# Moving adaLN slabs into the projections, splitting the output projection, and dummy products at the start

## The chip, the cores and the metric

One core of a Trainium2 chip runs the whole kernel. The time is the device time of one execution in microseconds; the median of several runs counts. TensorE is PE, VectorE is DVE, ScalarE is ACT, GpSimd is POOL; SP is the engine whose queue issues most DMAs.

## The reference, cut to what matters

Two layers of a hybrid decoder, for one prompt of 512 tokens and eight samples of 4 tokens (544 columns in all), model width 1024:

```python
mod = silu(c) @ w_ada + b_ada                    # 1024 -> 6*1024, per sequence
sh1, sc1, g1, sh2, sc2, g2 = split(mod, 6)
h = rms_norm(x, norm1) * (1 + sc1) + sh1
proj = h @ w_in                                  # q 512 | k 128 | v 128 | u 256 | xr 256 | yg 256
o_attn = window_attention(q, k, v, sinks)        # 8 heads, window 128
o_ssm = s5(u);  o_lru = rglru(xr, yg)            # two recurrent branches, 256 wide each
o = concat(rms_norm(o_attn), rms_norm(o_ssm), rms_norm(o_lru))
x = x + g1 * (o @ w_o)
h2 = rms_norm(x, norm2) * (1 + sc2) + sh2
x = x + g2 * ffn(h2)                             # up 1024 -> 2*2816, causal conv, gelu * value, down
```

New caches and states are returned as well.

## The kernel before, in words

**Layout.** Features lie on partitions (8 tiles of 128), tokens on columns, in two halves: `HALF` 0 has 256 columns, half 1 has 288 (256 of the prompt and the 32 of the samples). A float32 product is made of three products of a split in two parts (`mm3`, L427): `whi*hh`, `whi*hl`, `wlo*hh`. Weights come in tiles of 128x8x128 (512 KB) by a DMA on SP into one of `NRAW` = 3 buffers `raw`; ACT casts them to `whi`, DVE subtracts to get `wlo`, into one of `NW` = 6 slots (`Weights.ahead`, L407). `weights_order` (L1601) sets the order in which tiles are fetched; a new tile is fetched when a slot is given back (`done`).

**adaLN.** `ada_slabs` (L491) makes `mod`. A slab is 128 rows of `w_ada` by 1024 columns (512 KB): four matmuls of 32 columns of the silu against 256 columns each, into four row groups of one bank. 8 slabs make a sum; then ACT copies it, two transposes turn it, DVE adds the bias. There are 6 such sums, 48 slabs, in a layer. A slab's load takes a `raw` buffer of the weights' three, but for four slabs at the start that go to spare tiles in pieces of 512 bytes. At the start of layer 0 the slabs of `sh1` and `sc1` (16) run ahead of everything, fetched up to 7 ahead. The other 32 of layer 0 and the first 16 of layer 1 run as a background generator (list `bg`) between the products of the mixers of layer 0, the last 32 of layer 1 between those of layer 1, fetched one ahead. `background()` advances it, once or more per `tick`.

**A layer.** `mixers` (L1442): the 12 column tiles of `w_in`, each 8 k by 2 halves by 3 = 48 products; the first three run as a group over k as their normalised inputs appear (`group`, L877). Each tile's result starts a chain (`Chains`): k and q (norm, rotary), v, the S5 branch `ssm_chain`, the RG-LRU branch `lru_chain`. Attention is made of 16 units per layer, one step of a unit per tick: `att_S` (scores, exp), `att_T` (transposes), `att_V` (times v). `proj` (L1535): o @ w_o for 8 column tiles i and two halves; k tiles 6, 7 are the RG-LRU branch, 4, 5 the S5 branch, 0 to 3 attention. Its first three tiles run as a group over k in the order `KO`, and `need(k, hf)` ticks until an input is there:

```python
o = [one(256, True) for i in range(GRP)]
for k in ko:
    need(k, 0)
    for i in range(GRP):
        mm3(o[i], W_[wn(i)], k, hs[k], HALF[0], k == ko[0], k == ko[-1])
```

After it the tiles go through all k at once, in an order that runs half 0 four tiles ahead of half 1 (`skewed`). `residual` evicts a sum into x on DVE. `ffn` (L1614): 44 tiles of the up-projection (48 products each, then `conv`, and per pair gelu and split), and the down-projection in three parts (`PARTS`). `finish` (L1653) and `down` call `background()` once a tile; there only `tables` of the next layer is in the list. `norm_half` (L850) normalises, scales, shifts and splits one half of x for all k.

PSUM has 8 banks: `wide` (two pairs) always, four singles `mb` in the mixers, one pair and two singles `fb` in the projections.

Of the kernel before, what the change touches and what calls it, by code (L numbers as in the profile page):

```python
# [19 lines left out]
L = 2  # L20
# [29 lines left out]
S3 = 1  # L50
# [13 lines left out]

PRM = {}
_n = 0
for _name, _w in (
# [10 lines left out]
    "wada": (L, 3, 8, 2, 128, 4, 256), "win": (L, 12, 128, 8, 128), "wo": (L, 8, 128, 8, 128),  # L78
# [56 lines left out]
def layout(I):  # L135
# [43 lines left out]
    A["wada"] = I["w_ada"].reshape(L, 8, 128, 3, 4, 2, 256).transpose(0, 3, 1, 5, 2, 4, 6)  # L179
# [137 lines left out]
def trunk(ctx: ExitStack, tc: tile.TileContext, A, O):  # L317
# [173 lines left out]
    def ada_slabs(l, banks, ahead, spare=()):  # L491
        d = LY[l]
        todo = [(bank, k, hf) for bank in banks for hf in range(2) for k in range(8)]
        have = {}

        def fetch(n):
            if n < len(todo) and n not in have:
                bank, k, hf = todo[n]
                if n in spare:
                    have[n] = [T(512) for _ in range(2)]  # L500
                    for a, t in enumerate(have[n]):
                        nc.sync.dma_start(t.rearrange("p (g c) -> p g c", g=4),
                                          A["wada"][l, bank, k, hf, :, :, 128 * a:128 * a + 128])
                    return
                raw = wp.tile([128, 8, 128], F32, tag="raw", name="raw", bufs=NRAW)
                have[n] = raw.rearrange("p (g a) c -> p g (a c)", g=4)
                nc.sync.dma_start(have[n], A["wada"][l, bank, k, hf])

        for n, (bank, k, hf) in enumerate(todo):
            for m in range(n, n + ahead + 1):  # L510
                fetch(m)
            if k == 0:
                if bank == 0 and hf == 0:
                    d["mod"] = lp.tile([128, 48, 9], F32, name="mod")
                ps = one(256)
            if n in spare:
                for a, t in enumerate(have[n]):
                    for g in range(4):
                        T_.matmul(ps[32 * g:32 * g + 32, 128 * a:128 * a + 128], silu[:, k, :],
                                  t[:, 128 * g:128 * g + 128], start=False, stop=k == 7, skip_group_check=True)  # L520
                free(*have[n])
            else:
                for g in range(4):
                    T_.matmul(ps[32 * g:32 * g + 32], silu[:, k, :], have[n][:, g],  # L524
                              start=k == 0, stop=k == 7, skip_group_check=True)
            del have[n]
            yield 1
            if k < 7:
                continue
            row = W(256)  # L530
            S.copy(row, ps)
            PS.put(ps)
            yield 1
            pt = one(256)
            for c in range(2):
                T_.transpose(pt[:, c * 128:c * 128 + 128], row[:, c * 128:c * 128 + 128], eye)

            def part(t):
                return t[:, bank * 16:bank * 16 + 16].rearrange("p (g h c) r -> p g h c r", g=4, h=2)[:, :, hf]

            src = pt.rearrange("p (c g r) -> p g c r", c=2, g=4)[:, :, :, 0:9]
            b = d["prm"]("bada")[:, :, None].to_broadcast([128, 48, 9])
            V.tensor_tensor(part(d["mod"]), src, part(b), op=OP.add)
            PS.put(pt)
            d["ada"] = (bank, hf)
            for al, at, bk in (("al1", 8, 0), ("al2", 32, 2)):
# [319 lines left out]
    def norm_all(hf, al, sh):  # L866
        yield from norm_stats(hf)
        for _ in norm_half(hf, al, sh):
            pass
# [942 lines left out]
```

## Time and profile before

| | |
|---|---|
| median of 3 runs (lowest, highest) | 1330.35 us (1328.3, 1334.8) |
| the profiled execution, and its span | 1335.0 us, 1333.2 us |
| PE busy, weight loads (PEld) busy | 1270.1 us (95%), 1164.8 us (87%) |
| DVE, ACT, POOL busy | 881.8 (66%), 576.5 (43%), 48.8 us (4%) |
| mean granted TensorE clock | 0.992 of full speed |
| DMA | 178.24 MB, mean 134 GB/s |

Stages by the span's time: start to 62 us, mixers of layer 0 to 245, its output projection to 305, its up- and down-projection to 690, mixers of layer 1 to 893, its output projection to 945, its up- and down-projection to the end. A matmul's duration holds the time to its end, some 0.28 us; in a run of products one starts every 0.12 to 0.13 us, so busy time can look full where products start rarely. Weight loads overlap matmuls and show that better. A float32 matmul that isn't split appears as two instructions.

### The profile page before, as it was taken

Reading aid. Unit: us, or ns where it says so; the run is one execution under the profiler, and the core shown is the slowest. Engines: PE = TensorE matmul, PEld = TensorE weight load, DVE = VectorE, ACT = ScalarE, POOL = GpSimd, SP = SyncE. Lnnn points to the kernel's source line nnn. Section 1 sums busy time; section 2 is a strip of 40 time slices with the busy share of each in tenths; the row PEclk is TensorE's granted clock in tenths of the full one; section 3 lists DMA queues with packets and bytes.
Section 4 is the critical chain, followed back from the end, with each engine's and each line's share of the span. In section 5 each row is a group of like instructions: output and inputs, shape, how many; then the busy total and the mean of one; then the engine's idle time right before and its main releaser. Section 6 shows DMA issues by size and latency. Waiting matters only on the chain.

```text
span 1333.2 us, 26368 instructions
## 1 busy us (share of the span) xinstructions
PE 1270.1 (95%) x10438; PEld 1164.8 (87%) x10438; DVE 881.8 (66%) x2583; ACT 576.5 (43%) x1112; POOL 48.8 (4%) x82
## 2 busy tenths in 40 slices
PE   4899988999999999999999999899999999999998
PEld 2666765799999999999998776679999999999998
DVE  8787885988774556456576877668865456545651
ACT  4557544356542343234354466545643234313430
POOL 0021010000020000000000001000000000000000
PEclk9899999999999999999999999999999999999999
DMA  8876677533343223334235846602322332233221
GB/s 294 279 265 215 191 252 229 178 111 118 93 135 125 85 86 87 97 93 115 76 108 180 268 142 203 191 14 90 110 81 86 96 95 74 86 97 94 85 72 51
DMA packets 72460, 178.24 MB, mean 134 GB/s; under 512 B 15584, under 2 KB 26752, under 8 KB 72336
## 3 DMA queue, kind: packets, MB, share of 16 engines
q1 hardware_dynamic: 65456, 162.08, 39.1%
q0 software_dynamic: 4960, 11.68, 2.5%
q10 hardware_dynamic: 1920, 2.79, 0.7%
q8 instruction: 82, 1.34, 0.4%
q14 instruction: 42, 0.34, 0.1%
HBM read 159.37 MB, written 14.34 MB: 130 GB/s over the span
## 4 chain that ended last, share of the span: by engine, by line
PE 83%; DMA 9%; DVE 5%; ACT 2%; issue 1%; POOL 0%; SPq 0%; DVEq 0%; POOLq 0%; ACTq 0%
PE wide L430 42%; PE fb1w L430 9%; PE fb0w L430 8%; DMA raw<-in_wada_dram 6%; PE fb0s L430 5%; PE fb1s L430 4%; PE mb0s L430 3%; PE mb1s L430 3%; PE mb0s L524 1%; PE mb1s L524 1%; DMA raw<-in_wo_dram 1%; DVE wlo L416 1%; DMA f<-in_ssmh_dram 1%; DMA tab_br<-f 1%; PE mb1s L1242 0%
## 5 line engine op out<-in xcount | busy, mean ns | idle before, releaser
L430 PE MATMUL wide<-hh,whi 128*128 128x288 f32 (+1 forms) x1360 | 400.3, 295 | 1.2 <-ACT hh L897 0.8
L430 PE MATMUL wide<-hl,whi 128*128 128x288 f32 (+1 forms) x1360 | 395.9, 291 | 0.0
L430 PE MATMUL wide<-hh,wlo 128*128 128x288 f32 (+1 forms) x1360 | 394.3, 290 | 0.0
L416 DVE TENSOR_TENSOR wlo<-raw,whi 128x1024 fp32r<-128x1024 f32 (+1 forms) x176 | 211.0, 1200 | 187.1 <-ACT whi L415 183.1
L415 ACT CAST whi<-raw 128x1024 fp32r<-128x1024 f32 (+1 forms) x176 | 180.4, 1029 | 274.8 <-PE wide L430 125.8
L430 PEld LDWEIGHTS wide<-hh,whi 128*128 128x128 f32 x1360 | 257.2, 189 | 18.3 <-issue 14.0
L430 PEld LDWEIGHTS wide<-hl,whi 128*128 128x128 f32 x1360 | 257.1, 189 | 6.3 <-issue 6.1
L430 PEld LDWEIGHTS wide<-hh,wlo 128*128 128x128 f32 x1360 | 259.2, 191 | 3.0 <-issue 3.0
L380 DVE SCALAR_TENSOR_TENSOR f<-wide,prm,f 128x511 f32<-128x511 f32 x236 | 100.2, 485 | 0.0
L430 PE MATMUL wide<-mid,whi 128*128 128x256 f32 (+1 forms) x526 | 99.8, 287 | 0.0
L430 PEld LDWEIGHTS wide<-mid,whi 128*128 128x128 f32 x526 | 82.4, 188 | 0.0
L897 ACT CAST mid<-f 128x544 fp32r<-128x544 f32 x44 | 28.5, 647 | 122.4 <-DVE f L1660 119.1
L430 PE MATMUL wide<-mid,wlo 128*128 128x256 f32 (+1 forms) x263 | 75.5, 287 | 0.0
L377 ACT ACTIVATE f<-f 128x544 f32<-128x544 f32 x50 | 33.0, 659 | 89.2 <-DVE f L1650 84.5
L430 PE MATMUL fb1w<-hh,whi 128*128 128x256 f32 (+1 forms) x240 | 69.4, 289 | 1.8 <-ACT hh L862 1.3
L430 PE MATMUL fb1w<-hl,whi 128*128 128x256 f32 (+1 forms) x240 | 69.4, 289 | 0.0
L430 PE MATMUL fb1w<-hh,wlo 128*128 128x256 f32 (+1 forms) x240 | 68.8, 287 | 0.0
L430 PE MATMUL fb0w<-hh,whi 128*128 128x256 f32 (+1 forms) x224 | 64.7, 289 | 1.6 <-ACT hh L862 1.1
L430 PE MATMUL fb0w<-hl,whi 128*128 128x256 f32 (+1 forms) x224 | 64.7, 289 | 0.0
L430 PE MATMUL fb0w<-hh,wlo 128*128 128x256 f32 (+1 forms) x224 | 64.3, 287 | 0.0
L430 PE MATMUL fb0s<-mid,whi 128*128 128x288 f32 (+1 forms) x326 | 62.9, 290 | 0.0
L430 PE MATMUL fb1s<-mid,whi 128*128 128x288 f32 (+1 forms) x308 | 59.1, 289 | 0.0
(612 smaller groups left out, 2542.2 us busy)
## 6 DMA issues: line engine op xcount, KB each, us to landing
raw<-in_wada_dram SPq DMA_DIRECT2D x92, 512.0 KB, 5.2
raw<-in_wup_dram SPq DMA_DIRECT2D x88, 512.0 KB, 3.5
raw<-in_wdn_dram SPq DMA_DIRECT2D x32, 448.0 KB, 3.3
raw<-in_win_dram SPq DMA_DIRECT2D x24, 512.0 KB, 4.2
raw<-in_wo_dram SPq DMA_DIRECT2D x16, 512.0 KB, 4.5
raw<-in_wdn_dram SPq DMA_DIRECT2D x16, 512.0 KB, 3.5
e<-q ACTq DMA_DIRECT2D x32, 68.0 KB, 4.6
out_ox_dram<-x SPq DMA_DIRECT2D x8, 272.0 KB, 2.1
```

Of the source, the lines that this page charges most:

```text
L377: return S.activation(out, in_, f, bias=bias, scale=scale, **kw)
L380: return V.scalar_tensor_tensor(out, a, s, b, op0=op0, op1=op1, **kw)
L415: S.copy(hi, raw)
L416: V.tensor_sub(lo, raw, f32(hi))
L430: T_.matmul(out, w[wi][:, k, :], r[ri][:, a:b], start=first and i == 0, stop=last and i == 2)
L524: T_.matmul(ps[32 * g:32 * g + 32], silu[:, k, :], have[n][:, g], start=k == 0, stop=k == 7, skip_group_check=True)
L897: S.copy(dst[0], src)
```

## The change

- `w_ada` is cut into six parts per layer (`ADA`), the parts 0 and 1 for `sh1` and `sc1`, then `g1`, `sh2`, `sc2`, `g2`.
- **Early loads.** The 16 slabs of parts 0 and 1 of layer 0 are loaded before anything else runs, into tiles that the mixers use later (q, kz, xc, gate, glu), evictions' tiles and spare ones, five in `raw`. The mixers' tiles are made before (`mix_tiles`).
- **Dummies.** `warm(n)` puts n products of the ones matrix with itself (128x128) behind a slab, in program order: 32 in all, 24 of them between the first eight slabs, 8 behind the first sum.
- `ssm_rot` of layer 0 is issued after the first norm; the first half's norms of the layers use a form with one ACT pass fewer (`fast`).
- **Pairs.** Only parts 2 to 4 of layer 0 (24 slabs) stay in the mixers. Part 5 of layer 0 and all six of layer 1 (56 slabs) run as `ada_pairs` in the up-projection of layer 0: two slabs with one 1 MB load into a buffer of its own, one pair per `background()`, in a second list `bga`; `down` doesn't advance it. Layer 1's mixers have no slab.
- **Split output projection.** For column tiles 0 to 3 the products over k = 6, 7, 4, 5 run first, for both halves; sums are added into x apart from those over k = 0 to 3 (the three of the group keep one sum). Their weights come as two tiles of four k each.
- In `att_S` the copy of the sinks and the scaling by 1/sum go from DVE to ACT.

```diff
+WARM = {0: 2, 1: 3, 2: 3, 3: 3, 4: 3, 5: 3, 6: 3, 7: 4, 9: 8}
+WO = ((4, 8, range(4)), (0, 4, range(4)), (0, 8, range(4, 8)))
-AHEAD = 7
-SPARE = (4, 5, 9, 11)
-S12 = (2, 14, 5, 16)
+S12 = (2, 12, 5, 14)
-NHN = [9, 17]
+NHN = [9, 15]
+ADA = ([0, 2, 4, 6], [1, 3, 5, 7], [8, 9, 10, 11], [12, 13, 14, 15], [16, 17, 18, 19], [20, 21, 22, 23])
...
+    def ada_pairs(l, parts, raw, bank):
+        d = LY[l]
+        todo = [(part, k) for part in parts for k in range(0, 8, 2)]
+        def fetch(part, k):
+            nc.sync.dma_start(raw, A["wada"][l, part, k:k + 2].rearrange("k p g c -> p k g c"))
+        fetch(*todo[0])
+        yield 1
+        for n, (part, k) in enumerate(todo):
+            if k == 0:
...
+                ps = one(256, only=(bank,))
+            for i in range(2):
+                for g in range(4):
+                    T_.matmul(ps[32 * g:32 * g + 32], silu[:, k + i, :], raw[:, i, g],
+                              start=k + i == 0, stop=k + i == 7, skip_group_check=True)
+            if n + 1 < len(todo):
+                fetch(*todo[n + 1])
             yield 1
...
+            if k == 6:
+                yield from ada_end(l, part, ps)
...
+    def warm(n):
+        ps = one(128)
+        for _ in range(n):
+            tc.keep_in_program_order(T_.matmul(ps, ones, ones, start=True, stop=True))
+        PS.put(ps)
...
+            if fast and not hf:
+                hi, lo = (z[:, a:b] for z in hs[c])
+                stt(t, x[:, c, a:b], al[:, c, 0:1], nr, OP.mult, OP.mult)
+                act(hi, t, AF.Identity, bias=sh[:, c, 0:1])
+                stt(lo, t, sh[:, c, 0:1], f32(hi), OP.add, OP.subtract)
...
-        V.tensor_copy(pm[:, :, nk:nk + 1], d["nsink"][:, c, :, None])
+        S.copy(pm[:, :, nk:nk + 1], d["nsink"][:, c, :, None])
...
-            ts(pm[:, g, 0:nk], pm[:, g, 0:nk], st[:, 2, g:g + 1])
+            act(pm[:, g, 0:nk], pm[:, g, 0:nk], AF.Copy, scale=st[:, 2, g:g + 1])
...
         o = [one(256, True) for i in range(GRP)]
-        for k in ko:
+        for k in KO[:4]:
             need(k, 0)
             for i in range(GRP):
-                mm3(o[i], W_[wn(i)], k, hs[k], HALF[0], k == ko[0], k == ko[-1])
+                part(o[i], i, 0, k, k == KO[0], False)
+        for i in range(4):
+            for hf in range(2):
+                if (i, hf) not in ((0, 0), (1, 0), (2, 0)):
+                    some(i, hf, KO[:4], False)
+        for k in KO[4:]:
+            need(k, 0)
+            for i in range(GRP):
+                part(o[i], i, 0, k, False, k == KO[-1])
...
-                ad = ada_slabs(0, (0,), AHEAD, SPARE)
+                homes = [None] * 3 + [[M.q[i][:, :512], M.q[i + 1][:, :512]] for i in (0, 2)]
+                homes += [[M.kz[:, 0], M.kz[:, 1]], [t[:, :512] for t in M.xt],
+                          [M.gate.rearrange("p c j n -> p (c j n)"), M.glu.rearrange("p k n -> p (k n)")]]
+                have = {k: ada_load(0, 0, k, homes[k]) for k in range(8)}
+                W_.ahead(GRP)
+                fetch_x(1)
+                homes = [[E(512), E(512)] for _ in range(2)] + [[T(512), T(512)] for _ in range(4)]
+                for k in range(8):
+                    have[8 + k] = ada_load(0, 1, k, homes[k] if k < len(homes) else None)
+                ad = ada_slabs(0, (0, 1), 0, have)
...
-            bg.append(ada_slabs(l, (1, 2), 1))
+            if l == 0:
+                bg.append(ada_slabs(0, (2, 3, 4), 1))
             if l + 1 < L:
                 params(l + 1)
-                bg.append(ada_slabs(l + 1, (0,), 1))
...
+                raw = pool.tile([128, 2, 4, 256], F32, name="araw")
+                if l == 0:
+                    bga.append(ada_pairs(0, (5,), raw, "fb0s"))
+                bga.append(ada_pairs(l + 1, range(6), raw, f"fb{l}s"))
```

On PE, the first rows of the program were these before (`cin` is the silu of c; L524 and L519 are slabs, L459 and L478 the statistics of the first half of x, L536 the first sum's transposes):

```order
L524 MATMUL wide_70<-raw,cin 32x256 x8
L459 MATMUL wide_71<-eye,sqacc 128x128 x2
L524 MATMUL wide_70<-raw,cin 32x256 x8
L519 MATMUL wide_70<-f_89,cin 32x128 x4
L519 MATMUL wide_70<-f_90,cin 32x128 x4
L478 MATMUL mb0s_127<-eye,qr 128x128 x2
```

and are these now, with the dummies at L866:

```order
L552 MATMUL wide_70<-raw,cin 32x256 x4
L866 MATMUL wide_71<-ones 128x128 x2
L552 MATMUL wide_70<-raw,cin 32x256 x4
L866 MATMUL mb0s_127<-ones 128x128 x3
L461 MATMUL mb0s_128<-eye,sqacc 128x128 x2
L552 MATMUL wide_70<-raw,cin 32x256 x4
L866 MATMUL mb0s_129<-ones 128x128 x3
L552 MATMUL wide_70<-q,cin 32x256 x4
```

Behind each slab stand two to four dummies, and slabs come from tiles of the mixers (`q` here).

On SP, the loads of layer 0's last up-projection stretch stood in one row before:

```order
L412 DMA raw<-in_wup_dram 128x1024 x14
L412 DMA raw<-in_wdn_dram 128x1024
```

and alternate now with the pairs' loads (`araw`, 2x1024 columns):

```order
L414 DMA raw<-in_wup_dram 128x1024 x11
L567 DMA araw<-in_wada_dram 128x2x1024
L414 DMA raw<-in_wup_dram 128x1024
L567 DMA araw<-in_wada_dram 128x2x1024
L414 DMA raw<-in_wup_dram 128x1024
L567 DMA araw<-in_wada_dram 128x2x1024
L414 DMA raw<-in_wup_dram 128x1024
L567 DMA araw<-in_wada_dram 128x2x1024
L414 DMA raw<-in_wdn_dram 128x1024
```

Each `araw` load waits on SP until PE has read the pair before it; between most pairs stand the 48 products of one tile.

On PE, in the output projection of layer 0 (`hh_82` is k = 5, `hh_72` is k = 0, `hh_84` k = 6), the group went from k = 5 straight on to attention's k = 0:

```order
L430 MATMUL mb0s_128<-hh_82,whi_113 128x256
L430 MATMUL mb0s_128<-hl_83,whi_113 128x256
L430 MATMUL mb0s_128<-hh_82,wlo_114 128x256
L430 MATMUL wide_71<-hh_72,whi_109 128x256
L430 MATMUL wide_71<-hl_73,whi_109 128x256
```

and has the other tiles' products over k = 6, 7, 4, 5 there now:

```order
L432 MATMUL mb0s_128<-hh_82,wlo_114 128x256
L432 MATMUL mb0s_127<-hl_81,whi_109 128x288
L432 MATMUL mb0s_127<-hh_80,wlo_110 128x288
...
L432 MATMUL wide_71<-hh_84,whi_111 128x288
L432 MATMUL wide_71<-hl_85,whi_111 128x288
...
L432 MATMUL mb0s_127<-hh_82,wlo_116 128x256
L432 MATMUL wide_71<-hh_72,whi_117 128x256
```

So five groups of 12 products moved ahead of the first product that needs attention.

## Rows read from the trace of the kernel before

**Rows 1.** Busy us (x records) by stage: PE, PEld, DVE, ACT, POOL; clock, DMA share, GB/s.

```profile
192.00:245.00 53.00, 44.35 (x432) 26.17 (x432) 33.80 (x146) 23.44 (x67) 1.94 (x2) 0.94 0.75 245
...
305.00:690.00 385.00, 384.50 (x3120) 383.28 (x3119) 232.24 (x504) 148.97 (x246) 11.48 (x21) 1.00 0.33 99
690.00:840.00 150.00, 141.67 (x1228) 115.23 (x1227) 113.31 (x358) 86.76 (x178) 10.51 (x14) 0.99 0.64 196
840.00:893.00 53.00, 46.52 (x376) 33.47 (x376) 37.44 (x145) 27.54 (x82) 0.00 (x0) 1.00 0.32 102
```

**Rows 2.** The same for the slabs' line L524 alone: PE, PEld, clock, DMA, GB/s.

```profile
62.00:192.00 130.00, 18.77 (x192) 4.85 (x192) 1.00 0.72 225
192.00:245.00 53.00, 15.28 (x168) 4.42 (x168) 0.94 0.75 245
245.00:305.00 60.00, 1.92 (x24) 0.47 (x24) 1.00 0.40 129
...
690.00:840.00 150.00, 18.63 (x192) 4.58 (x192) 0.99 0.64 196
840.00:893.00 53.00, 5.71 (x64) 1.82 (x64) 1.00 0.32 102
```

**Rows 3.** PE's waits: us in total, times, longest us.

```profile
PE wide L524 <- DMA raw<-in_wada_dram: 12.0, 5, 8.9
PE mb0s L524 <- DMA raw<-in_wada_dram: 11.0, 9, 2.4
PE mb1s L524 <- DMA raw<-in_wada_dram: 9.3, 10, 1.7
```

**Rows 4.** The chain that ended last: start us, us, what.

```profile
201.68 6.04 DMA raw<-in_wada_dram
...
457.00 12.01 PE wide L430 x96
```

**Rows 5.** PE in order of time, the start: start us, us, what [idle before, releaser].

```profile
20.97 1.08 PE L524 MATMUL wide<-raw,cin 128*32 128x256 f32 x8 [0.19 <-DMA raw<-in_wada_dram]
...
27.50 0.58 PE L430 MATMUL mb0s<-hh,whi 128*128 128x256 f32 x1 [4.21 <-ACT hh L862]
...
33.27 0.41 PE L430 MATMUL mb0s<-hh,wlo 128*128 128x256 f32 x1
...
33.77 0.28 PE L430 MATMUL wide<-hh,wlo 128*128 128x256 f32 x1
...
48.63 1.08 PE L524 MATMUL mb0s<-raw,cin 128*32 128x256 f32 x8
...
55.07 0.28 PE L430 MATMUL mb0s<-hh,whi 128*128 128x256 f32 x1
```

**Rows 6.** Rate of the loads: the page's 40 slices, and a 2 us stretch by engine.

```profile
GB/s 294 279 265 215 191 252 229 178 111 118 93 135 125 85 86 87 97 93 115 76 108 180 268 142 203 191 14 90 110 81 86 96 95 74 86 97 94 85 72 51
...
8.00:10.00 2.00, 1.06 (x8) 0.23 (x8) 1.90 (x9) 1.96 (x4) 0.00 (x0) 1.00 1.03 414
```

**Rows 7.** DVE groups by line and shape: busy us, mean ns, idle before.

```profile
L380 DVE SCALAR_TENSOR_TENSOR x<-wide,mod,x 128x256 f32<-128x256 f32 x44 | 21.3, 483 | 47.9 <-PE wide L430 47.9
...
L384 DVE TENSOR_SCALAR pm<-pm,st 128x256 f32<-128x256 f32 x48 | 14.9, 348 | 0.3
```

**Rows 8.** PE in order of time, one slab between products.

```profile
782.92 0.29 PE L430 MATMUL wide<-hh,wlo 128*128 128x288 f32 x1
783.14 0.64 PE L524 MATMUL mb1s<-raw,cin 128*32 128x256 f32 x8
...
783.94 0.28 PE L430 MATMUL wide<-hl,whi 128*128 128x256 f32 x1
```

**Rows 9.** DMA issues: count, KB each, median us from issue to landing.

```profile
raw<-in_wada_dram SPq DMA_DIRECT2D x92, 512.0 KB, 5.2
raw<-in_wup_dram SPq DMA_DIRECT2D x88, 512.0 KB, 3.5
```

More of the change, by code (lines that the diff above doesn't have):

```diff
@@ new lines, in ada_load @@
+    def ada_load(l, part, k, homes=None):
+        src = A["wada"][l, part, k]
+        if homes:
+            v = [t.rearrange("p (g c) -> p g c", g=2) for t in homes]
+            for a, t in enumerate(v):
+                nc.sync.dma_start(t, src[:, 2 * a:2 * a + 2])
+            return v
+        raw = wp.tile([128, 8, 128], F32, tag="raw", name="raw", bufs=NRAW)
+        t = raw.rearrange("p (g a) c -> p g (a c)", g=4)
+        nc.sync.dma_start(t, src)
+        return [t[:, 0:2], t[:, 2:4]]
@@ L496, in fetch, with ada_slabs @@
+    def ada_slabs(l, parts, ahead, have=None):
+        d = LY[l]
+        todo = [(part, k) for part in parts for k in range(8)]
+        have = have or {}
         def fetch(n):
             if n < len(todo) and n not in have:
[L498 to L504, printed above, removed]
@@ L530, in ada_slabs @@
[L530 to L542, printed above, removed]
@@ L543, in ada_slabs @@
[L543 to L546, printed above, removed]
-                if bk == bank:
-                    alpha(l, al, "norm" + al[2], at, hf)
-            yield 1
+            if k == 6:
+                yield from ada_end(l, part, ps)
     def alpha(l, al, n, at, hf):
@@ L1466, in mixers @@
             setattr(M, n, const(n, sh, pool=pool))
+        return M
+    def mixers(l, M):
+        d = LY[l]
+        mod = d["mod"]
+        sh1 = mod[:, 0:8]
+        M.win_done = M.back = False
+        M.units, M.pipe, M.left = ([], []), [None, None], [8, 9]
+        M.r, M.o, M.g, M.hl = {}, set(), [None, None], [None, None]
+        M.sq, M.part = {}, {}
+        for g in range(2):
+            G.memset(M.kz[64 - 64 * g:128 - 64 * g, g], 0.0)
+        AR.names.update((t.tensor.name, t) for t in M.xt)
         CH = M.CH = Chains()
@@ L1510, in mixers @@
             ssm_params(0)
-            for _ in ssm_rot(0):
-                pass
+            with tc.issue_after(LY[0]["first"]):
+                for _ in ssm_rot(0):
+                    pass
             t0 = ssm_tables(0, 0)
@@ L1549, in need, with part, end @@
             raise RuntimeError(("never ready", k, hf, M.left))
-        def end(i, hf, o):
+        def part(o, i, hf, k, first, last):
+            a = 0 if i > 3 or k < 4 else 4
+            mm3(o, W_[("wo", l, a, i)], k - a, hs[k], HALF[hf], first, last)
+        def end(i, hf, o, last=True):
             with urgent():
@@ L1566, in proj @@
         for i, hf in skewed(GRP):
-            for k in range(KC):
-                need(k, hf)
-            a, b = HALF[hf]
-            o = one(b - a, True, PLAST[0] if (i, hf) in PLAST[1] else ())
-            for k in ko:
-                mm3(o, W_[wn(i)], k, hs[k], HALF[hf], k == ko[0], k == ko[-1])
-            end(i, hf, o)
-            tick()
+            some(i, hf, KO if i > 3 else KO[4:])
             if (i, hf) == (7 - SKEW, 1):
```

140 lines of the change are left out of this document (78 added, 62 removed).

## The prediction

> **What bounds the kernel now.** I read the views in this order: busy time by stage, then the same stages for the slabs of `w_ada` alone, TensorE's (PE's) waits, the chain that ended last, and at last the order of time on PE at three places.
>
> In the stage table [rows 1] the up- and down-projection of layer 0 (305 to 690) is PE and nothing else: 384.5 us busy of 385, weight loads 383.3. The two mixer stages look nearly as full, but their weight loads tell another story: 26.2 us of 53 from 192 to 245, 115.2 of 150 from 690 to 840. There PE is held by waits in its own order of work, and VectorE (DVE) is busy 113.3 of 150.
>
> What holds it is to a good part the slabs [rows 2]. A slab is eight MATMUL records in the trace, so the counts give 24 slabs from 62 to 192, 21 from 192 to 245, 3 from 245 to 305, 24 from 690 to 840 and 8 from 840 to 893. None lies in a projection stage. A slab is work for PE (0.6 to 0.8 us of busy time each), and a wait too: PE waited 12.0, 11.0 and 9.3 us for `in_wada` to land [rows 3], 8.9 of the 12.0 before the first slab of all. Those waits are in PE's queue, so all that stands behind a slab is late with it. In the chain a single slab transfer takes 6.04 us of its own [rows 4]. A slab shares the three `raw` buffers with the weights, so its load can't start before a buffer is given back.
>
> The start is a matter of loads [rows 5]: the eighth slab is consumed at 20.97, the first product starts at 27.50, the sixteenth slab is consumed at 48.63, and the products that need it start at 55.07. The products before 33.3 take 0.41 us (1.2 GHz), those after 0.28 (2.4 GHz).
>
> **The change part by part.** All is summed against the profiled execution of 1335.0 us (its span is 1333.2); the median of the runs shown is 1330.35, so the result is carried over as a difference.
>
> *Early loads and dummies (start).* The sixteenth slab is behind about 12.5 MB, by the shapes: 5.6 MB up to the eighth slab (parameters, half of x, eight slabs of 512 KB), three weight tiles of 512 KB, the other half of x (1.2 MB), eight slabs more (4.2 MB). In the first of the 40 slices the loads ran at 294 GB/s, and in a stretch without a held load at 414 [rows 6]. No load of a slab now waits for a buffer in use, but for the last two. So the sixteenth slab lands between 2 + 12.5/0.414 = 32 and 2 + 12.5/0.294 = 44.5 us; I take 39, nearer to the fast end since the loads are of 2 KB and 4 KB rows in place of 512 bytes. The chain behind it is the 6.4 us from 48.63 to 55.07, as before. Products that need it then start at 45.5: **−9 us**, with bounds −4 and −15. The statistics of the second half of x and its norm stand on the same way and keep me from the lower end. `ssm_rot` moves behind the first norm on DVE; the wait for slabs nine to sixteen covers it, so I set it at nothing, and without that cover the −9 shrinks to its bound of −4. The 32 dummies lie between slabs that PE waits for; if the clock rises they cost nothing, otherwise see the fourth rival.
>
> *24 slabs out of mixer 0.* The 24 that stay are as many as now lie before 192, so that stretch keeps its length. From 192 to 245 PE has 44.35 us of work, of it 15.28 slabs [rows 1, 2]; without them 29.1, and 7.5 us of output projection come in (below): 36.6 is the least, 53 the most if attention's own chain is as long as the stretch. I take 42: **−11**. It is nearer to the low end because slabs and their transfers are what PE waits for there. From 245 to 305 go 1.9 us of slabs.
>
> *The split output projection.* Of its 384 products per layer, 36 could run before attention is ready; now it is 96, since half of k (the two recurrent branches) is done for four column tiles. A product takes 12.01/96 = 0.125 us [rows 4], so 60 products, 7.5 us, leave the stage after attention for the one before, in both layers. So 245 to 305 falls by **9.4** (1.9 + 7.5), and 893 to 945 by **7.5**. The price: five evictions more per layer on DVE, of 0.483 us [rows 7], and four more weight tiles through the six slots. DVE is idle a third of the time from 192 to 245 and hides them, so I set both at nothing; without that cover it is 2.4 us a layer.
>
> *32 slabs out of mixer 1.* From 690 to 840 PE has 141.67 us of work, 18.63 of it slabs: 123 is the least, 140.7 the most (the 9.3 us of direct waits alone go). DVE's 113.3 us must fit too, so I take 130: **−20**. From 840 to 893: 46.52 − 5.71 + 7.5 = 48.3 at least; I take 49: **−4**.
>
> *56 slabs into the projections of layer 0, in 28 pairs.* PE has no gap there, so all of it is paid. A slab set between products makes 1.02 us of what would be 2 × 0.125 [rows 8]: 0.77. The second one of a pair adds its 0.64: 1.41 a pair, 39.5 for 28, and 2.5 for seven sets of two transposes: **+42**.
>
> *The wait of a pair.* One buffer of 1 MB holds a pair; its next load starts when PE has read the last, and 20 of the 28 pairs stand only 48 products, 6.0 us, behind the one before. A 512 KB weight tile lands in 3.5 us in these stages, a slab in 5.2 in the crowded ones [rows 9]. So 1 MB takes between 3.5 and 10.4 us. I take 5.3: 3.5 plus another half megabyte at 294 GB/s. That leaves some 0.7 us of slack for the hop of a semaphore, and I put **+2** for the cases that meet a weight load. Weights queued behind a pair's load on SP are nine tiles ahead of PE, so they don't starve.
>
> By the Trainium skill (DMA: Bandwidth & Descriptors, section Bandwidth) a measured 1 MB load, issued from GpSimd, keeps the DMA engines busy for 6.15 us. If that holds here, each of the 20 pairs would wait about half a microsecond, the +2 would be about +9, and the median about 1320.
>
> *Small moves.* The 64 scalings of the attention weights go from DVE (0.348 us [rows 7]) to ScalarE, which has the room (23.4 of 53 us busy); attention's chain gains or loses less than 0.3 us per unit. The first half's norm loses a ScalarE pass; nothing waits for it long.
>
> Sum: −9 − 11 − 9.4 − 20 − 4 − 7.5 + 42 + 2 = **−17** us; 1335.0 becomes 1318, the median 1330.35 becomes **1313**.
>
> **The rivals.**
> 1. *PE work alone decides in the mixers.* Attention and the recurrent chains had only been held up by slabs. Then the mixers fall to their least values, the start gives 12 and no pair waits: −12 − 16.4 − 9.4 − 27 − 4.7 − 7.5 + 42 = −35, **1295**. For it: the weight loads' share [rows 1]. Against it: DVE at three quarters.
> 2. *The chains are the limit and slabs only filled their gaps.* Then 192 to 245 gives 5, 690 to 840 gives 12, the other small ones stay, the start gives 6: −6 − 5 − 9.4 − 12 − 2 − 7.5 + 44 = +2: **1332**, no change. For it: from 192 to 245 PE has no products to run (20 of them in 53 us), and the slabs there were filler. Against it: PE stood in front of unlanded slabs with work behind them.
> 3. *The pair's load is late* (the slower side). The place is PE's queue in the up-projection, the price what a load takes beyond 5.7 us, twenty times, in a stage that nothing else slows now. At 6.7 us of landing it has eaten the gain, from 7.0 the kernel is slower by over 0.5%; at 7.8 it is 20 × 2.1 = 42 in place of 2: **1353**. For it: the slab's 5.2 us for half the size. Against it: most of those loads were in stages at 196 to 245 GB/s, and here it is 99 [rows 1] plus what the pairs add.
> 4. *The dummies don't do what they are for.* If PE stays at 1.2 GHz, the 24 between slabs are paid on the way to the first product at about 0.5 us each (half a slab's 1.1 us), and the start gains nothing: −8, **1322**.
>
> **How the numbers follow.** The forecast has 0.47, the first rival 0.20, the second 0.14, the third 0.13, the fourth 0.06. About 0.5% (6.7 us) is what a measurement of this kernel can tell from no change. Faster by more than that, under 1323.7: the forecast, the first rival and half of the fourth, less the forecast's slow tail: 0.69. Slower, above 1337: the third and a tail of the second: 0.14. The rest, 0.17, is the same. The range is 1290 to 1337: its low end holds the first rival, its high end the second, and outside it lie most of the third rival and what is lower than the first.
>
> **What will show it.** In the after profile the stage table should show the output projection of layer 0 end near 276 in place of 305, the projections of layer 0 last about 430 us in place of 385, and layer 1's mixers about 224 us in place of 255. PE's waits for `raw<-in_wada` should be below 10 us beyond the start, and those for `araw` below 5. Products behind the sixteenth slab should start near 45 us. The forecast is wrong if `araw` stands at the head of PE's waits with 20 us or more, if layer 1's mixers are longer than 240 us without a single slab in them, or if the first product starts later than 27.5.

## The result, and the profile after

The changed kernel is slower: 1347.03 us median of 4 runs (1344.7 to 1348.53) beside 1332.57 us for the kernel before on the same chip, ratio **1.0114** [1.0086, 1.0142]. The forecast was 1313 us, faster. The profiled execution took 1347.11 us, its span is 1345.3 us, 12.1 us more than the span before.

The stage table of the kernel before, cut where the last product of a stage stands (columns as in [rows 1]; two stages a layer, w_in with all that runs beside it and the output projection, then up and down):

```profile
67.00:192.00 125.00, 116.27 (x1034) 88.58 (x1026) 103.38 (x410) 74.60 (x164) 17.36 (x29) 1.00 0.72 226
192.00:294.00 102.00, 93.35 (x827) 73.29 (x828) 75.83 (x289) 43.03 (x108) 4.14 (x6) 0.97 0.58 188
...
698.00:843.00 145.00, 136.67 (x1187) 109.69 (x1185) 108.30 (x344) 81.20 (x163) 9.47 (x12) 0.99 0.63 195
843.00:929.00 86.00, 79.39 (x635) 66.32 (x634) 65.12 (x233) 44.15 (x118) 0.00 (x0) 1.00 0.30 94
```

The same of the changed kernel, the projections of layer 0 among them:

```profile
64.00:190.00 126.00, 118.98 (x1043) 89.56 (x1036) 100.46 (x396) 87.78 (x210) 19.09 (x32) 1.00 0.71 225
190.00:278.00 88.00, 80.89 (x628) 69.85 (x629) 74.56 (x280) 45.93 (x109) 3.22 (x4) 0.92 0.32 101
278.00:725.00 447.00, 439.68 (x3728) 417.06 (x3727) 255.86 (x582) 163.73 (x277) 12.15 (x23) 1.00 0.46 154
725.00:844.00 119.00, 112.20 (x965) 99.92 (x964) 95.90 (x304) 78.34 (x167) 10.38 (x14) 1.00 0.40 115
844.00:941.00 97.00, 87.05 (x585) 72.55 (x586) 70.68 (x231) 57.19 (x154) 0.00 (x0) 0.89 0.21 62
```

Layer 1's w_in stage lost 26 us with its slabs, as hoped, but the output projection behind it *grew* by 11 us although PE has 50 fewer records there; its granted clock fell from 1.00 to 0.89, and ACT is busy 57.19 us in place of 44.15. From the order of products on PE (each stage ends with the end of its last product; `start` ends with the first three tiles of w_in), in us, of profiled executions that lie within 5 us of their kernel's median:

| kernel | start | w_in 0 | out 0 | up/down 0 | w_in 1 | out 1 | rest |
|---|---|---|---|---|---|---|---|
| before | 66.9 | 124.7 | 102.7 | 403.8 | 144.8 | 85.7 | 404.6 |
| **changed** | 63.8 | 125.9 | 88.8 | 446.3 | 119.1 | 97.0 | 404.4 |
| changed, scalings on VectorE (e1) | 64.5 | 129.2 | 89.5 | 445.7 | 114.1 | 93.3 | 404.4 |
| changed, no pairs (e4) | 63.6 | 129.0 | 104.8 | 408.4 | 149.0 | 91.9 | 406.6 |
| changed, scalings on VectorE, no dummies, unsplit (e6) | 57.5 | 128.4 | 90.2 | 443.8 | 116.1 | 91.0 | 407.7 |
| before, pairs alone (e7) | 67.1 | 123.7 | 95.2 | 435.9 | 115.6 | 89.0 | 404.3 |
| before, scalings alone (e9) | 66.2 | 123.6 | 103.8 | 403.8 | 146.6 | 91.5 | 404.4 |
| before, split alone (e10) | 67.1 | 123.0 | 100.0 | 407.2 | 142.0 | 89.8 | 404.1 |
| before, pairs and late slabs (e15) | 67.8 | 116.9 | 97.3 | 423.1 | 115.6 | 94.0 | 404.0 |

PE's waits after (as [rows 3]) and the loads' issues after (as [rows 9]):

```profile
PE wide L552 <- DMA raw<-in_wada_dram: 9.8, 1, 9.8
PE fb0s L578 <- DMA araw<-in_wada_dram: 5.1, 4, 3.0
PE mb0s L552 <- DMA raw<-in_wada_dram: 3.4, 5, 1.5
```

```profile
raw<-in_wup_dram SPq DMA_DIRECT2D x88, 512.0 KB, 3.5
araw<-in_wada_dram SPq DMA_DIRECT2D x28, 1024.0 KB, 5.1
```

So the waits for slabs behind the first sum fell from 20.3 us (11.0 and 9.3 in [rows 3]) to 3.4, and the pairs wait 5.1 us in all. Neither is where the time went.

### The profile page after: what moved, and what is told of

Read it like the earlier page. It is cut to its first block, busy times and chain, and to the rows that moved or that the text cites. A ratio compares the mean times of both kernels' runs of the same rounds, so it can differ in the third digit from the quotient of the medians.

```text
span 1345.3 us, 26372 instructions
## 1 busy us (share of the span) xinstructions
PE 1284.3 (95%) x10470; PEld 1180.3 (88%) x10470; DVE 871.9 (65%) x2521; ACT 601.6 (45%) x1198; POOL 48.8 (4%) x82
## 3 DMA queue, kind: packets, MB, share of 16 engines
q8 instruction: 82, 1.34, 0.4%
## 4 chain that ended last, share of the span: by engine, by line
PE 64%; DVE 4%; DMA 3%; ACT 2%; issue 1%; POOL 0%; SPq 0%; DVEq 0%; POOLq 0%; ACTq 0%
PE wide L432 33%; PE fb1w L432 9%; PE fb0w L432 7%; PE fb1s L432 4%; PE mb1s L432 3%; PE fb0s L432 3%; DMA araw<-in_wada_dram 2%; PE fb0s L578 2%; PE mb1s L1290 1%; ACT pm L379 1%; PE mb1s L1129 1%; DMA f<-kscr 0%; DVE f L382 0%; ACT whi L417 0%; PE mb1s L1311 0%
## 5 line engine op out<-in xcount | busy, mean ns | idle before, releaser
L432 PE MATMUL wide<-hh,whi 128*128 128x256 f32 (+1 forms) x1368 | 401.3, 294 | 5.5 <-ACT whi L417 2.3
L432 PE MATMUL wide<-hl,whi 128*128 128x256 f32 (+1 forms) x1368 | 396.8, 290 | 0.0
L432 PE MATMUL wide<-hh,wlo 128*128 128x256 f32 (+1 forms) x1368 | 395.7, 289 | 0.7 <-DVE wlo L418 0.7
L418 DVE TENSOR_TENSOR wlo<-raw,whi 128x1024 fp32r<-128x1024 f32 (+2 forms) x184 | 212.1, 1153 | 194.3 <-ACT whi L417 190.4
L417 ACT CAST whi<-raw 128x1024 fp32r<-128x1024 f32 (+2 forms) x184 | 182.3, 991 | 306.9 <-PE wide L432 174.0
L432 PE MATMUL wide<-mid,whi 128*128 128x256 f32 (+1 forms) x582 | 112.7, 291 | 0.0
L432 PEld LDWEIGHTS wide<-mid,whi 128*128 128x128 f32 x582 | 92.6, 191 | 0.5 <-issue 0.5
L945 ACT CAST mid<-f 128x544 fp32r<-128x544 f32 x44 | 28.5, 647 | 126.3 <-DVE f L1726 123.0
L432 PE MATMUL wide<-mid,wlo 128*128 128x256 f32 (+1 forms) x291 | 84.4, 290 | 0.0
L382 DVE SCALAR_TENSOR_TENSOR x<-wide,mod,x 128x256 f32<-128x256 f32 x53 | 25.6, 483 | 66.2 <-PE wide L432 66.1
L379 ACT ACTIVATE pm<-pm,st 128x256 f32<-128x256 f32 (+3 forms) x128 | 57.2, 476 | 10.7 <-DVE st L1292 6.5
```

Source lines behind the costliest of these rows:

```text
L379: return S.activation(out, in_, f, bias=bias, scale=scale, **kw)
L382: return V.scalar_tensor_tensor(out, a, s, b, op0=op0, op1=op1, **kw)
L417: S.copy(hi, raw)
L418: V.tensor_sub(lo, raw, f32(hi))
L432: T_.matmul(out, w[wi][:, k, :], r[ri][:, a:b], start=first and i == 0, stop=last and i == 2)
L945: S.copy(dst[0], src)
```

## The experiments

Each ratio is to the kernel before on the same chip, with its 95% interval; 0.001 is 1.33 us.

### One part of the changed kernel undone

**e1, the scalings back on VectorE.**

```diff
-            act(pm[:, g, 0:nk], pm[:, g, 0:nk], AF.Copy, scale=st[:, 2, g:g + 1])
+            ts(pm[:, g, 0:nk], pm[:, g, 0:nk], st[:, 2, g:g + 1])
```

(and the copy of the sinks likewise).

> The changed kernel with one part undone: the copy of the sinks and the 64 scalings of the attention weights go back from ScalarE to VectorE. Theory A (attention's own chain of steps sets the pace: in layer 1 it took 102.7 us from its first scores to its last product with v before and 103.5 after, although 32 slabs had gone): the pace doesn't hang on which engine scales, so 100 to 106 us again and a total of 1344 to 1350. Rival B (the scalings lengthened attention, two ScalarE passes of about 0.48 us a unit in place of two VectorE passes of 0.35, on an engine that is busy 13.5 of 17 us just then): first scores to last product falls to 95 or less, the total to 1335 to 1340.

Measured: 1342.58 us, **1.0054** [1.0034, 1.0074], 8 us less than the changed kernel's ratio. Rival B holds in layer 1, a little short of the sizes that it named. First scores and last product with v there, in the order of time on PE, of the kernel before, 102.9 us to the end of the last:

```profile
790.65 0.70 PE L1242 MATMUL mb1s<-kz,q 128*128 128x256 f32 x2
...
892.89 0.66 PE L1277 MATMUL mb1s<-f,vt 128*64 128x128 f32 x8
```

of the changed kernel, 103.7 us:

```profile
801.65 0.70 PE L1290 MATMUL mb1s<-kz,q 128*128 128x256 f32 x2
...
904.73 0.66 PE L1325 MATMUL mb1s<-f,vt 128*64 128x128 f32 x8
```

and of e1, 96.1 us:

```profile
805.42 0.70 PE L1290 MATMUL mb1s<-kz,q 128*128 128x256 f32 x2
...
900.82 0.66 PE L1325 MATMUL mb1s<-f,vt 128*64 128x128 f32 x8
```

**e2, no dummies** (`WARM = {}`).

> The changed kernel without the 32 dummy products. If they raise the clock in time for the first products: the eight slabs run at about 1.08 us each in place of 0.64, first product at about 28 us as before since the norm, not the slabs, is what it waits for; total within 3 us of 1347. If they hold the first norm up: first product 2 to 4 us earlier, total 1343 to 1345. If the clock matters for what follows: granted clock falls in the first 30 us and the total rises to 1350 to 1353.

Measured: 1339.74 us, **1.0044** [1.0023, 1.0065], 9 us less. None of the three readings had that total; the second had the first product right. The start in the changed kernel (last slab of the first sum, dummies, first product, last slab of the second sum; columns as in [rows 5]):

```profile
22.12 0.39 PE L552 MATMUL wide<-glu,cin 128*32 128x256 f32 x2
22.44 1.16 PE L866 MATMUL mb0s<-ones 128*128 128x128 f32 x8
23.43 0.38 PE L502 MATMUL wide<-eye,half 128*128 128x128 f32 x2
23.65 1.95 PE L866 MATMUL mb0s<-ones 128*128 128x128 f32 x16
27.93 0.38 PE L432 MATMUL wide<-hh,whi 128*128 128x256 f32 x1 [2.33 <-ACT whi L417]
...
48.61 0.64 PE L552 MATMUL mb0s<-raw,cin 128*32 128x256 f32 x8
```

and in e2 (an execution 5.2 us above its median):

```profile
19.09 0.62 PE L552 MATMUL wide<-glu,cin 128*32 128x256 f32 x4
20.25 0.44 PE L502 MATMUL wide<-eye,half 128*128 128x128 f32 x2 [0.53 <-ACT half L497]
24.81 0.58 PE L432 MATMUL wide<-hh,whi 128*128 128x256 f32 x1 [4.12 <-DVE wlo L418]
...
46.01 0.71 PE L552 MATMUL mb0s<-raw,cin 128*32 128x256 f32 x8
```

The dummies did keep the clock up: the first products take 0.38 us with them and 0.58 without, and from 25 to 30 us the granted clock is 1.00 (2.4 GHz) with and 0.50 (1.2 GHz) without, behind a wait of 4.12 us. But PE worked without a break from 9.8 to 25.6 us. The slabs had landed, so the dummies stood on the way to the first sum: its transposes came at 23.43 in place of 20.25, the first product 3.1 us later. What follows stays 2.5 us later to the end of the first three tiles (63.8 and 61.3).

**e3, the projection unsplit**: all eight k of a tile at once, eight weight tiles, as before.

> The changed kernel with the output projection of before (all eight k at once, eight weight tiles). Forecast's view (60 products, 7.5 us, leave the stretch behind attention in each layer): 7 to 15 us slower, 1354 to 1362. Rival D (in layer 0 the recurrent branches are ready no earlier than attention, so nothing moves ahead; in layer 1 the moved products stand in PE's queue between attention's steps and delay them: from the first product of the projection to attention's last one 44.2 us after, 37.2 before): that stretch of layer 1 falls by 5 to 8 us, what follows grows by as much or less, and the total is 1340 to 1348.

Measured: 1348.02 us, **1.0101** [1.0061, 1.0140]: no difference from the changed kernel beyond the intervals. Theory D's two halves both show. In layer 0, 24 products of the projection run before attention's last product with v in e3 as in the changed kernel, so the split moves none there. In layer 1 from the projection's first product to attention's last one 38.7 us in place of 44.2; behind that 34.8 us with 257 products left, and 35.6 us with 216 when split. Why 41 products fewer (5 us) save nothing shows on PE behind attention's last product, in the changed kernel:

```profile
908.66 0.28 PE L432 MATMUL mb1s<-hh,wlo 128*128 128x256 f32 x1
910.53 0.43 PE L480 MATMUL wide<-eye,qr 128*128 128x128 f32 x2 [1.59 <-DVE qr L382]
912.00 0.61 PE L432 MATMUL mb1s<-hh,whi 128*128 128x288 f32 x1 [1.04 <-ACT hh L945]
...
913.24 0.61 PE L432 MATMUL mb1s<-hl,whi 128*128 128x288 f32 x1 [0.15 <-DVE hl L946]
...
913.89 0.44 PE L432 MATMUL mb1s<-hh,whi 128*128 128x288 f32 x1
```

and in e3:

```profile
911.90 0.28 PE L432 MATMUL mb1s<-hh,wlo 128*128 128x256 f32 x1
912.01 0.29 PE L432 MATMUL wide<-hh,whi 128*128 128x288 f32 x1
912.41 0.43 PE L480 MATMUL wide<-eye,qr 128*128 128x128 f32 x2
...
913.22 0.29 PE L432 MATMUL wide<-hh,wlo 128*128 128x288 f32 x1
```

Unsplit, products of the first half cover the last norm of attention. Split, they ran earlier; PE waits for the norm, and the clock falls. The stretch just behind the wait in the changed kernel (columns as in [rows 1]):

```profile
908.00:912.00 4.00, 1.37 (x12) 0.93 (x10) 3.76 (x18) 0.90 (x3) 0.00 (x0) 0.95 0.00 0
912.00:918.00 6.00, 5.85 (x23) 5.50 (x24) 4.52 (x14) 2.65 (x5) 0.00 (x0) 0.50 0.00 0
```

6 us at 1.2 GHz, a product every 0.24 us, after 4 us with 1.37 us of work.

**e4, no pairs**: the 56 slabs back in the mixers, singly.

```diff
-            if l == 0:
-                bg.append(ada_slabs(0, (2, 3, 4), 1))
+            bg.append(ada_slabs(l, (2, 3, 4, 5), 1))
             if l + 1 < L:
                 params(l + 1)
+                bg.append(ada_slabs(l + 1, (0, 1), 1))
...
-                if l == 0:
-                    bga.append(ada_pairs(0, (5,), raw, "fb0s"))
-                bga.append(ada_pairs(l + 1, range(6), raw, f"fb{l}s"))
```

> The changed kernel with the 56 slabs of the pairs back in the mixers, singly, through the weights' buffers: parts 5 of layer 0 and 0, 1 of layer 1 behind the 24 in layer 0's mixers, parts 2 to 5 of layer 1 in layer 1's. Theory A (a slab was worth less where it stood, about 14 us for 32 in layer 1, than the 0.76 us it costs in the up-projection): the projections of layer 0 fall from 446 to 404 us, the mixers with their output projections grow by 12 to 14 us in each layer, total 1330 to 1335. Forecast's view (some 1 us a slab in the mixers): total 1345 or more.

Measured: 1353.99 us, **1.0158** [1.0117, 1.0199], slower still. This is against my theory A: I had begun to blame the pairs, and taking them away costs rather than gives. By the table the projections fall by 37.9 us, and the four mixer stages grow by 43.9. So some 20 us of loss lie in the other parts.

### Parts undone together

**e5** is e1 and e2 together.

> The changed kernel with two parts undone at once: the scalings of attention back on VectorE, and no dummies. The scalings alone gave back 8 us (ratio 1.0054 in place of 1.0114), the dummies 9 (1.0044). If these are two separate costs, the sum is about 1.0114 - 0.0060 - 0.0070 = 0.998 of the time before: 1330 to 1335 beside 1335, and layer 1's attention takes 94 to 98 us from first scores to last product. If the gain without dummies was an accident of the order that the scheduler found, only the scalings' gain remains: 1338 to 1343.

Measured: 1334.78 us, **1.0001** [0.9969, 1.0033]: the two costs add (0.998 worked out).

**e6** is e5 with e3's projection.

> The run before it, and the output projection of before (unsplit). Alone that edit changed the total by less than its interval (1.0101 in place of 1.0114): in layer 1 the stretch behind attention's last product took 35.6 us split with 216 products left and 34.8 unsplit with 257, because the split leaves PE idle for some 5 us while the last norm is made, and the stretch before it is 5 us shorter unsplit. Theory D (moved products cover nothing and uncover the norm): within 4 us of the run before it, either way. Forecast's view (7.5 us a layer): 10 to 15 us slower.

Measured: 1337.27 us, **1.0018** [0.9987, 1.0049]: the split is worth nothing here either.

### One part alone on the kernel before

**e7, pairs alone**: 24 pairs for layer 1, the same generator and 1 MB buffer; the 32 slabs of layer 0 stay.

```diff
-            bg.append(ada_slabs(l, (1, 2), 1))
+            if l == 0:
+                bg.append(ada_slabs(l, (1, 2), 1))
             if l + 1 < L:
                 params(l + 1)
-                bg.append(ada_slabs(l + 1, (0,), 1))
...
+                bga.append(ada_pairs(l + 1, range(3), raw, f"fb{l}s"))
```

> The kernel before with one part of the change alone: the 48 slabs of layer 1 as 24 pairs in the up-projection of layer 0, with the 1 MB buffer of its own; layer 0's 32 stay in its mixers, all else as before. From the stage times of the changed kernel with and without pairs: projections of layer 0 plus 24 x 1.5 = 36 us; layer 1's mixers and output projection minus 23 to 25; layer 0's minus 8 to 11 (16 of the 24 that went there). Theory: within 5 us of before, 0.998 to 1.003. Forecast's own sum for this part alone (minus 8, minus 24, plus 36): about plus 4 as well; a loss of 10 us or more would put the pairs themselves to blame.

Measured: 1328.36 us, **0.9966** [0.9941, 0.9990]: a small gain, just better than the 0.998 to 1.003 expected. Projections of layer 0 +32.1 us (1.34 a pair), layer 1's two mixer stages -25.9, layer 0's -8.5. Layer 1's attention took 93.1 us in place of 102.9.

**e9, the scalings alone**: the reverse of e1's edit, on the kernel before.

> The kernel before with one part of the change alone: the copy of the sinks and the 64 scalings of the attention weights on ScalarE. If the cost that undoing it gave back (about 8 us, most of it in layer 1: attention there 103.5 us with it, 95.8 without) belongs to this part by itself: layer 1's first scores to last product from 102.7 to 108 to 112 us, total 1.004 to 1.008 of before. If it costs only where slabs no longer fill PE (before, a step of attention is held by slabs as well): 0.999 to 1.003.

Measured: 1343.18 us, **1.0065** [1.0041, 1.0089]. Layer 1's attention on PE, 111.9 us; before it was 102.9 (lines at e1):

```profile
788.52 0.70 PE L1242 MATMUL mb1s<-kz,q 128*128 128x256 f32 x2
...
899.72 0.66 PE L1277 MATMUL mb1s<-f,vt 128*64 128x128 f32 x8
```

**e10, the split alone**: `proj` and `WO` of the change on the kernel before.

> The kernel before with one part alone: the split output projection with its two sorts of weight tiles. The forecast counted 7.5 us a layer for it: 0.989 of before. Theory D (what moves ahead of attention comes back as an uncovered norm and as products between attention's steps): 0.997 to 1.004.

Measured: 1338.04 us, **1.0021** [1.0001, 1.0042]. Behind attention's last product PE waits 1.59, 1.04 and 0.58 us for the norm here too, in a kernel that has its slabs in the mixers.

**e11, the early loads alone**: e6 without pairs, as in e4.

> The early loads alone, without dummies (the changed kernel with the pairs, the split, the scalings and the dummies undone; the shorter norm of the first half stays): slabs go back to the mixers as in the run without pairs. The group of the first three tiles of w_in should end near 58 to 60 us in place of 66.9. If that gain lasts: 0.993 to 0.996 of before. If w_in's stage gives it back (with the same three parts undone and pairs it took 128 to 131 us in place of 124.7): 0.998 to 1.002.

Measured: 1334.53 us, **1.0022** [0.9990, 1.0053]. The start ended at 60.6 in place of 66.9 (58 to 60 expected), so 6 us were gained there and nothing in the total. Its profiled execution stands 14 us above its median, so where they are given back can't be read from it.

**e13, the dummies alone**: `warm` and `WARM` on the kernel before.

> The kernel before with one part alone: the 32 dummies at the same places between its first slabs (its loads stay as they are, so PE still waits for a slab after most of them). If dummies cost only where slabs have already landed, as in the changed kernel (continuous PE work from 9.8 to 25.6 us there, first product 3 us later than without): here the waits hold most of them, first product at 27.5 to 29, total 0.999 to 1.002 of before. If they cost something beyond the start (7 to 9 us measured with the early loads, 3 of them seen at the start): 1.004 or more.

Measured: 1333.56 us, **1.0006** [0.9980, 1.0032]. Where PE waits for slabs anyway, dummies cost nothing that the interval shows, though the first product came at 29.31 in place of 27.50. They gain nothing either: from 30 to 50 us the granted clock is 0.50 to 0.55, where in the kernel before a product took 0.41 us (1.2 GHz) until 33.3 [rows 5], and the clock was 0.50 to 0.54 again from 40 to 50.

**e14, e6 with the dummies put back.**

> The run with the scalings on VectorE, without dummies and unsplit (1.0018 of before), with the dummies put back: pairs, early loads and dummies are in. A third measurement of the dummies in the changed kernel: if they cost 7 to 9 us, 1.007 to 1.009; if only the 3 us that the start shows, 1.003 to 1.005.

Measured: 1344.82 us, **1.0084** [1.0053, 1.0115]. With e2 and e5 that is three comparisons of the dummies beside early loads: 0.0070 ± 0.0035, 0.0053 ± 0.0038 and 0.0066 ± 0.0044, some 8 us. The start shows 2.5 to 4.4 us of them. The rest isn't located.

### Slabs where PE waits for attention

**e8**: e6, and parts 4 and 5 of each layer behind the last product of w_in, with loads up to two ahead, the first of them issued before that product; 16 pairs stay.

```diff
+            bgl.append(ada_slabs(l, (4, 5), 2, None, True))
...
+                    if M.win_done:
+                        background(min(n, 4), (bgl,))
```

> The run without dummies, with the scalings on VectorE and the projection unsplit, and 32 slabs moved into the stretch where PE waits for attention: parts 4 and 5 of each layer are issued only behind the last product of w_in, up to four a tick, loads up to two ahead in the weights' buffers; 8 slabs fewer in layer 0's w_in stage, 16 pairs in place of 28 in the projections. If that stretch has idle PE time to give: the projections of layer 0 fall by 12 x 1.5 = 18 us, the stretch behind w_in grows by 3 to 8 in each layer, total 1318 to 1328, faster than both kernels. If slabs and their loads there delay attention's steps as they did before: the growth is 10 us or more a layer, total 1332 to 1340.

Measured: 1329.11 us, **0.9951** [0.9926, 0.9977], faster than both kernels, if 1 us above the range. Beside e6 the projections of layer 0 fell by 20.4 us and layer 1's two mixer stages grew by 6.2, as the first reading had it; layer 0's output projection grew by 10.4, and its w_in stage fell by 4.2.

**e12**: 8 slabs more there (part 3 of layer 1), 12 pairs.

> The run with 32 slabs behind w_in, and 8 more: parts 3, 4 and 5 of layer 1 there, 12 pairs in the up-projection in place of 16. There a slab cost about 0.4 us (16 slabs: layer 1's two stages 213.3 us in place of 207.0), in the up-projection 0.7. If there is idle time left: 2 to 3 us less than that run, 0.992 to 0.995 of before. If the 16 had used it up: the same as that run or up to 3 us more, 0.995 to 0.998.

Measured: 1330.82 us, **0.9978** [0.9949, 1.0006]: no gain beyond e8's, as the second reading had it; the two intervals overlap.

**e15**: the same idea without any other part: e7 with 16 pairs in place of 24, and the last 16 slabs of each layer behind w_in.

```diff
-                bg.append(ada_slabs(l, (1, 2), 1))
+                bg.append(ada_slabs(l, (1,), 1))
+            bgl.append(ada_slabs(l, (2,), 2, (), True))
...
-                bga.append(ada_pairs(l + 1, range(3), raw, f"fb{l}s"))
+                bga.append(ada_pairs(l + 1, range(2), raw, f"fb{l}s"))
```

> The kernel before, with 16 pairs for layer 1's first 32 slabs in the up-projection, and the last 16 slabs of each layer behind w_in as in the run with slabs there; start, projection and scalings as before. That run had 0.9951 with the early loads in it; alone they cost 1.0022 of before, so without them 0.990 to 0.995 is expected, the fastest of all. If the early start is needed for it: 0.996 to 1.000.

Measured: 1321.83 us, **0.9913** [0.9883, 0.9942], the lowest ratio of all and faster than both kernels; its interval overlaps e8's. Its output projection of layer 1 beside that of e7 without late slabs. e7:

```profile
838.00:927.00 89.00, 81.81 (x601) 68.45 (x602) 70.89 (x250) 48.72 (x132) 0.00 (x0) 0.98 0.15 44
```

e15:

```profile
821.00:915.00 94.00, 91.60 (x733) 71.19 (x734) 72.33 (x256) 49.57 (x134) 0.00 (x0) 1.00 0.41 131
```

9.8 us more PE work, and 5 us more time: 0.31 us for each of 16 slabs. In the projections they cost 12.8 us (435.9 to 423.1), 0.80 each. They aren't free: attention there took 98.0 us in place of e7's 93.1, which is all of the 5 us. The 16 late slabs of layer 0 gained too: its two mixer stages are some 5 us shorter than e7's. So of the places tried here a slab was cheapest behind w_in, where PE waits for attention.

## Why the prediction was wrong

The sum was -17 us; the span came out at +12. By the stretches that the sum was made of, cut by the products on PE (one profiled execution each, us; `attention` is from w_in's last product to the last product with v, `behind` from there to the output projection's last):

| stretch | before | changed | difference | forecast |
|---|---|---|---|---|
| start | 66.9 | 63.8 | -3.1 | -9 |
| w_in 0 | 124.7 | 125.9 | +1.1 | 0 |
| attention 0 | 50.7 | 39.0 | -11.6 | -11 |
| behind 0 | 52.1 | 49.7 | -2.3 | -9.4 |
| up/down 0 | 403.8 | 446.3 | +42.5 | +42 and +2 |
| w_in 1 | 144.8 | 119.1 | -25.7 | -20 |
| attention 1 | 50.6 | 61.5 | +11.0 | -4 |
| behind 1 | 35.1 | 35.5 | +0.4 | -7.5 |
| rest | 404.6 | 404.4 | -0.2 | 0 |

The pairs and w_in 1 came out near or better. The -11 did in part by luck: it let 60 products of the projection in, and 6 came. Four rows missed, and three steps of the prediction stand behind them.

**Right in mechanism: the slabs and the pairs.** Alone (e7) the slabs gave -25.9 in layer 1 and -8.5 in layer 0. The forecast's -20 and -4, and -8.6 for 16 of layer 0's 24 slabs, look the same; but its -11 and -4 hold the split's 7.5 us coming in. With those counted out it had -31.5 and -13.6, some 10 us too much. A pair was forecast at 1.41 us and its share of the transposes, +42 for 28, and came to +32.1 for 24 with its waits; the stage in the changed kernel grew by 42.5. The pair's wait, put at +2, was 5.1; 1 MB landed in 5.1 us, where I had taken 5.3. The third rival, a late load on every pair, did not happen. The 6.15 us of the Trainium skill (DMA: Bandwidth & Descriptors, section Bandwidth) would have made the wait +9: the median here is 5.1, and four loads were late. By the pairs alone the kernel is a little faster, as in e7.

**Wrong: "60 products, 7.5 us, leave the stage after attention for the one before, in both layers".** Split alone is 1.0021, about +3 us, and behind attention layer 1 took 35.9 us with it in place of 35.1, not 7.5 less. Two steps failed. First the count: "36 could run before attention is ready". By the order on PE before, 126 products of layer 1's projection already ran before attention's last product with v, since the first half of the columns needs only its own half of attention; the split makes them 168. In layer 0 it moves none (18 before and in e10, 24 in the changed kernel and in e3): the S5 branch (k = 4, 5) is ready there no sooner than attention, whose last product with v ended at 242.3 before, while the first product with the S5 branch started at 243.6. Second, what moves was cover. The products of the first half stood over attention's last norm, and without them PE waits 2.8 us (1.59, 1.04, 0.15; 3.2 us in e10) and then runs 6 us at the lower clock. I had asked what hides each added step, and not what each moved step had hidden.

**Wrong: "attention's chain gains or loses less than 0.3 us per unit".** It lost 0.56 us a unit in layer 1 (e9: 111.9 us in place of 102.9, 16 units), and that is on the path, since the output projection waits for attention: e9's total is 1.0065, +9 us. (In layer 0 attention took no longer in e9, 153.6 us beside 154.2; why, no run shows.) The pass itself explains about half:

```profile
L379 ACT ACTIVATE pm<-pm,st 128x256 f32<-128x256 f32 x48 | 21.8, 501 | 1.4 <-DVE st L1299 1.1
```

501 ns on ACT beside 348 on DVE [rows 7], twice a unit. I had looked at ACT's share (23.4 of 53 us) and concluded room. A chain asks for latency, and on ACT the scaling stands in one queue behind the exponentials, copies and squares of its neighbours; that this makes the other half is argued, not shown. The Trainium skill (Trainium Architecture — The Big Picture, section The five engines, in one table) lists simple arithmetic as what ScalarE is not for; these rows agree, 501 to 348.

**Wrong: "-9 us" for early loads and dummies.** The products behind the sixteenth slab started at 53.6, not 45.5:

```profile
53.63 0.28 PE L432 MATMUL mb0s<-hh,whi 128*128 128x256 f32 x1
```

The landing was well guessed (39; in the trace it is at 37.9): DMA moved 188 GB/s from 35 to 40 us and nothing from 40 to 45 (columns as in [rows 1]):

```profile
35.00:40.00 5.00, 5.00 (x21) 2.64 (x21) 4.04 (x27) 0.00 (x0) 0.00 (x0) 0.50 0.47 188
40.00:45.00 5.00, 3.59 (x31) 1.64 (x27) 2.01 (x10) 1.89 (x5) 0.00 (x0) 0.88 0.00 0
```

But the sixteenth slab is in PE's queue behind products that wait for the second half's norm (the first of them started at 44.96), and PE read it at 48.61 (line at e2). Held so, slabs also kept their `raw` buffers: in SP's waits up to 60 us, 10.8 us went by until PE had read one and the next weight could be loaded:

```profile
SPq L414 <- PE mb0s L552: 12.2, 2, 10.8
```

"The 32 dummies lie between slabs that PE waits for" was true of the kernel before, where they cost nothing that shows (e13), and not of the change, whose early loads had taken those waits away. Two parts were each costed against the kernel before, and one removes the other's cover. Without dummies the start is 5.6 to 9.4 us shorter than before (e2, e6), and still the total gains nothing (e11): e6's w_in stage of layer 0 takes 128.4 us in place of 124.7, and e8 with early loads ends it at 183.4, e15 without them at 184.6. What bounds w_in there stays open.

The single parts add up within their intervals, though e7's pairs and slabs are not quite the change's: pairs -0.0034, scalings +0.0065, split +0.0021, early loads +0.0022, and dummies beside early loads +0.0063 make +0.0137 ± 0.006; measured +0.0114 ± 0.0028. None of the four rivals is this: the fourth had the dummies on the way to the first product, but by a clock that didn't rise, and none had attention lengthened.

Of the signs that the text named, the projections of layer 0 fit (+42.5 us, +45 forecast). The output projection of layer 0 ended 16 us earlier, not 29, and layer 1's two stages are 14.4 us shorter, not 31. (The text cut the stages at 305, 690 and 945 us; by the products they end at 294, 698 and 929.) One sign of being wrong came true: the first product started at 27.93, later than 27.5. What I didn't name was the one that told: attention's length in layer 1, hardly changed by 32 slabs fewer (102.9 and 103.7 us), because the scalings took back what the slabs gave (111.9 in e9 with the scalings alone, 93.1 in e7 with the slabs alone).

## What to carry to other kernels

Before you move work earlier, look at what it was covering where it stood, and cost two parts of a change against each other as well as against the kernel before. Work on a chain is priced by what it adds to the chain, its pass and the queue that it joins, not by the share of time that engine is busy. Filler that must run somewhere belongs where PE waits with no other work: in e15 a slab cost 0.31 us there and 0.80 in a full stage, and PE's granted clock in that stretch was 1.00 in place of 0.98.

## What the runs showed of the hardware

After 2.8 us of waits PE ran 6 us at 1.2 GHz in the full flow of products (0.24 us a product in place of 0.13). That is some 3 us more, so by this estimate the wait cost about twice its length. Behind the dummies, which ended at 25.6 us, the granted clock was 1.00 from 25 to 30 us and 0.93 to 35, and 0.50 from 35 to 40; without them (e2) it was 0.50 from 25 to 35. In e13 it lay at 0.50 to 0.55 from 30 to 50 us; without them PE ran at 1.2 GHz until 33.3 us (0.41 us a product [rows 5]) and again, at 0.50 to 0.54, from 40 to 50. The mean granted clock of the changed kernel, 0.983, was below the 0.992 before, although dummies had been added.
